# W_down's product as seven products of quarters, with sums of W_down's quarters parked in DRAM

## The chip, the cores and the metric

One core of a Trainium2 chip runs the whole layer; everything is float32 at the interface. The metric is the device time of one execution in microseconds (us), lower is better. Engines are named as in the profile: PE (matrix product), PEld (its weight loads), DVE, ACT, POOL (the compute engines beside it) and SP (which here only issues DMAs).

## The reference, cut to what matters

One layer of a decoder: an attention and convolution block (unchanged here) and then a SwiGLU block and a final norm. The last two lines are what the change touches; S = 512 rows, D_MODEL = 1024, D_FF = 2816.

```python
h = h + mix @ w_o[l]
n = rmsnorm(h, g_ffn[l])
h = h + (jax.nn.silu(n @ w_gate[l]) * (n @ w_up[l])) @ w_down[l]
return rmsnorm(h, g_final)
```

With A = silu(n W_gate) * (n W_up), of 512 x 2816, the change is about A W_down, where W_down is 2816 x 1024.

## The kernel before

**Three products for one.** PE multiplies in fp32r. Each operand is split into a high part (rounded to fp32r by ACT: `wh`, `nH`, `aH`) and a low part (the operand less its high part, by DVE: `wl`, `nL`, `aL`). The helper `mm` (L119 to L121) issues three matmuls for each tile product: high by high, then the two of high and low. `wchunk` loads a weight chunk of 128 x 1024 with a DMA from SP into `raw` and splits it into `wh` and `wl`; `raw`, `wh` and `wl` have three buffers each, so that a chunk's split can run once PE has left the chunk three before it.

**The end of the program, in order.** The product with W_o and the second norm give n in transposed form as `nH`, `nL` (8 tiles of 128 x 512). Then comes gate and up: for each of the FT = 22 tiles ft of D_FF, 24 matmuls of 512 columns with a chunk of W_gate and 24 with a chunk of W_up, each into a PSUM bank (eight of them, `acc`); `ffn_act` (L912) then makes silu (ACT), the product (DVE, L915), and the split of the result into `aH`, `aL` (ACT L916, DVE L917). Its first three chunks are split early into space that `aH` and `aL` take later (`early_chunk`). Then W_down: `wd_mm` (L932) takes an A tile as the stationary operand and W_down's chunk as the moving one, first for the left 512 output columns and all four row tiles t, then for the right 512. `add_sq` adds to `h1` and sums the squares, `var` and a POOL power make 1/rms, and `scale_out` scales and stores.

**Order.** PE's order is the one in which the code is written. The other engines' instructions are ordered ahead of time by a list scheduler; each engine then runs its own list strictly in order, waiting at semaphores. DMAs issued from SP, ACT or POOL stand in that engine's list as well.

Of the kernel before, what the change touches and what calls it, by code (L numbers as in the profile page):

```python
# [51 lines left out]
def trace(tc, a):  # L52
# [879 lines left out]
    def wd_mm(ps, w, fc, t, c0, n):  # L932
        ts_ = slice(t * P, (t + 1) * P)
        for ff in range(2):
            k = 2 * fc + ff
            c = slice(ff * 512 + c0, ff * 512 + c0 + n)
            mm(ps, (aH[:, k, ts_], aL[:, k, ts_]), (w[0][:, c], w[1][:, c]),
               k == 0, k == FT - 1)

    def add_sq(ps, t, cs, q):  # L940
        nc.vector.tensor_tensor(h1[:, t, cs], ps, h1[:, t, cs], op=ALU.add)
# [9 lines left out]
    NF = FT // 2  # L951
    half = slice(0, 512)
    pss = [acc.tile([P, S], F32, name="acc") for _ in range(NT)]
    for fc in range(NF):
        w = wchunk(a["wd"][0, fc], eng=nc.vector)
        for t in range(NT):
            wd_mm(pss[t], w, fc, t, 0, 512)
    for t in range(NT):
        add_sq(pss[t], t, half, 0)
        var(t, 0, EPS)  # L960
        nc.gpsimd.tensor_tensor(h1[:, t, half], h1[:, t, half], gfin[:, half], op=ALU.mult)  # L961


    parts = [(t, 0, 512) for t in range(3)] + [(3, 0, 256), (3, 256, 256)]
    pss = [acc.tile([P, S], F32, name="acc") for _ in parts]

    def part(i, ws, f0):
        t, c0, n = parts[i]
        for q, w in enumerate(ws):
            wd_mm(pss[i][:, 0:n], w, f0 + q, t, c0, n)  # L970

    for fc in range(NF - 2):
        w = wchunk(a["wd"][1, fc], eng=nc.vector)
        for i in range(5 if fc < NF - 3 else 3):
            part(i, [w], fc)
    ws = [w] + [wchunk(a["wd"][1, fc], eng=nc.vector) for fc in range(NF - 2, NF)]

    rest = slice(512, D)

    def scale_out(t):  # L980
        r = st[:, t, 1:2]
        lo, hi = h1[:, t, half], h1[:, t, rest]
# [7 lines left out]
        nc.sync.dma_start(a["out_0"][t][:, rest], hi)  # L990

    for i, (t, c0, n) in enumerate(parts):
        if i < 3:
            part(i, ws[1:], NF - 2)
        else:
            part(i, ws, NF - 3)
        q = 1 if i < 4 else 2
        add_sq(pss[i][:, 0:n], t, slice(512 + c0, 512 + c0 + n), q)
        if i in (1, 2, 4):
            scale_out(t - 1)  # L1000
        var(t, q, st[:, t, 0:1])
        if i != 3:
            nc.gpsimd.tensor_tensor(st[:, t, 1:2], st[:, t, 0:1], mhalf[:, 0:1], op=ALU.pow)
# [74 lines left out]
```

## Time and profile before

| | us |
|---|---|
| median of 3 runs | 919.27 |
| lowest, highest | 918.22, 921.02 |
| the profiled execution, its own time | 917.53 |
| its span, first to last instruction | 915.7 |
| PE busy in the span | 898.8 (98%) |

The profiled execution is one run of its own: its time lies 1.74 us below the median of the three, and 1.83 us of it lies outside the span. Instruction times in the trace count from the span's start. A busy share says how long an engine had an instruction in hand, not that it ran at its best rate.

### The profile page before, as it was taken

Reading aid. Unit: us, or ns where it says so; the run is one execution under the profiler, and the core shown is the slowest. Engines: PE = TensorE matmul, PEld = TensorE weight load, DVE = VectorE, ACT = ScalarE, POOL = GpSimd, SP = SyncE. Lnnn points to the kernel's source line nnn. Section 1 sums busy time; section 2 is a strip of 40 time slices with the busy share of each in tenths; the row PEclk is TensorE's granted clock in tenths of the full one; section 3 lists DMA queues with packets and bytes.
Section 4 is the critical chain, followed back from the end, with each engine's and each line's share of the span. In section 5 each row is a group of like instructions: output and inputs, shape, how many; then the busy total and the mean of one; then the engine's idle time right before and its main releaser. Section 6 shows DMA issues by size and latency. Waiting matters only on the chain.

```text
span 915.7 us, 12776 instructions
## 1 busy us (share of the span) xinstructions
PE 898.8 (98%) x4757; PEld 760.2 (83%) x4757; DVE 515.5 (56%) x1217; ACT 426.3 (47%) x936; POOL 119.6 (13%) x79
## 2 busy tenths in 40 slices
PE   9889999999999999999999999999999999999996
PEld 7789788888888888878888999888888888888885
DVE  4896788888888788775455452333333333223223
ACT  6446776767767777664333522332223222212212
POOL 1000424232242222330000300000000000000100
PEclk9999999999999999999999999999999999999999
DMA  9244511211112111114523700223333323332212
GB/s 313 70 119 162 161 47 50 67 47 53 65 46 71 47 52 65 47 64 150 178 92 97 235 16 24 93 92 92 100 108 92 92 93 103 102 94 92 93 47 92
DMA packets 26270, 85.14 MB, mean 93 GB/s; under 512 B 3424, under 2 KB 3680, under 8 KB 26208
## 3 DMA queue, kind: packets, MB, share of 16 engines
q1 hardware_dynamic: 24912, 82.78, 28.5%
q10 hardware_dynamic: 1296, 1.55, 0.5%
q8 instruction: 37, 0.61, 0.3%
q14 instruction: 25, 0.20, 0.1%
HBM read 82.23 MB, written 2.10 MB: 92 GB/s over the span
## 4 chain that ended last, share of the span: by engine, by line
PE 88%; DVE 6%; DMA 2%; ACT 2%; issue 1%; SPq 0%; POOL 0%; POOLq 0%; ACTq 0%; DVEq 0%
PE acc L119 24%; PE acc L121 24%; PE acc L120 24%; PE sc L497 4%; PE tp L564 4%; PE av L582 2%; PE av L583 2%; DVE blk L249 2%; DVE wl L96 1%; PE av L577 1%; DMA w2kr<-w2k 1%; DMA raw<-wk 1%; ACT wh L95 1%; DMA xT<-xT 0%; DMA xt<-x 0%
## 5 line engine op out<-in xcount | busy, mean ns | idle before, releaser
L95 ACT ACTIVATE wh<-raw 128x1024 fp32r<-128x1024 f32 (+2 forms) x143 | 144.6, 1013 | 314.4 <-PE acc L120 117.0
L119 PE MATMUL acc<-nH,wh 128*128 128x512 f32 x656 | 262.3, 400 | 0.0
L121 PE MATMUL acc<-nH,wl 128*128 128x512 f32 x656 | 256.1, 390 | 0.0
L120 PE MATMUL acc<-nL,wh 128*128 128x512 f32 x656 | 256.1, 390 | 0.0
L96 DVE TENSOR_TENSOR wl<-raw,wh 128x1024 fp32r<-128x1024 f32 (+2 forms) x107 | 123.4, 1154 | 170.1 <-ACT wh L95 170.0
L121 PEld LDWEIGHTS acc<-nH,wl 128*128 128x128 f32 x656 | 123.1, 188 | 26.8 <-POOL wl L96 0.4
L119 PEld LDWEIGHTS acc<-nH,wh 128*128 128x128 f32 x656 | 123.4, 188 | 21.4
L120 PEld LDWEIGHTS acc<-nL,wh 128*128 128x128 f32 x656 | 123.5, 188 | 21.2
L96 POOL TENSOR_TENSOR wl<-raw,wh 128x1024 fp32r<-128x1024 f32 x36 | 86.6, 2407 | 236.7 <-DVE pt L540 96.4
L121 PE MATMUL acc<-wh,aL 128*128 128x512 f32 (+1 forms) x198 | 73.4, 371 | 0.0
L119 PE MATMUL acc<-wh,aH 128*128 128x512 f32 (+1 forms) x198 | 73.4, 371 | 0.0
L120 PE MATMUL acc<-wl,aH 128*128 128x512 f32 (+1 forms) x198 | 73.4, 370 | 0.0
L524 ACT ACTIVATE pt<-pt,nm 128x128 f32<-128x128 f32 (+3 forms) x128 | 70.7, 554 | 2.6 <-DVE nm L509 2.0
L509 DVE CUSTOM_DVE_ANT_0 pt<-sc,tri,nrs 128x128 f32<-128x128 f32 (+3 forms) x128 | 65.4, 545 | 0.1
L568 DVE TENSOR_TENSOR tl<-tp,th 128x512 fp32r<-128x512 f32 x80 | 55.1, 689 | 13.0 <-ACT th L567 11.3
L915 DVE TENSOR_TENSOR sg<-acc,sg 128x512 f32<-128x512 f32 x22 | 15.2, 691 | 81.0 <-PE acc L121 81.0
L567 ACT ACTIVATE th<-tp 128x512 fp32r<-128x512 f32 x80 | 47.4, 592 | 13.2 <-PE tp L564 12.1
L564 PE MATMUL tp<-ident,pt 128*128 128x128 f32 x320 | 49.7, 277 | 0.1
L961 POOL TENSOR_TENSOR h<-h,gfin 128x512 f32<-128x512 f32 x4 | 6.0, 1542 | 299.1 <-ACT jk L943 299.1
L120 PEld LDWEIGHTS acc<-wl,aH 128*128 128x128 f32 x198 | 37.3, 188 | 7.1
L119 PEld LDWEIGHTS acc<-wh,aH 128*128 128x128 f32 x198 | 37.3, 188 | 7.1
L121 PEld LDWEIGHTS acc<-wh,aL 128*128 128x128 f32 x198 | 37.3, 188 | 7.0
(229 smaller groups left out, 1496.9 us busy)
## 6 DMA issues: line engine op xcount, KB each, us to landing
raw<-wg SPq DMA_DIRECT2D x22, 512.0 KB, 3.5
raw<-wu SPq DMA_DIRECT2D x22, 512.0 KB, 3.5
raw<-wd SPq DMA_DIRECT2D x22, 512.0 KB, 3.5
raw<-wcv SPq DMA_DIRECT2D x12, 512.0 KB, 3.6
raw<-wq SPq DMA_DIRECT2D x8, 512.0 KB, 3.6
raw<-w SPq DMA_DIRECT2D x8, 512.0 KB, 3.5
raw<-wgc SPq DMA_DIRECT2D x8, 512.0 KB, 3.5
raw<-wga SPq DMA_DIRECT2D x8, 512.0 KB, 3.5
```

Of the source, the lines that this page charges most:

```text
L95: nc.scalar.activation(h[:, :n], raw[:, :n], AF.Copy)
L96: ins = (eng or nc.gpsimd).tensor_tensor(l[:, :n], raw[:, :n], f(h[:, :n]), op=ALU.subtract)
L119: nc.tensor.matmul(ps, lhs[0], rhs[0], start=first, stop=False)
L120: nc.tensor.matmul(ps, lhs[0], rhs[1], start=False, stop=False)
L121: nc.tensor.matmul(ps, lhs[1], rhs[0], start=False, stop=last)
L249: nc.vector.tensor_tensor(blk[lp * HD:(lp + 1) * HD, :, 2 * ct + hp, 0:NB - 1], src, pos, op=ALU.add)
L497: nc.tensor.matmul(o, q[:, h, qs], kk[g // 2][:, g % 2, c0:c0 + n], start=(j == 0), stop=(j == 1))
L509: nc.vector.tensor_tensor_reduce(out=pt[:, r0:r0 + w].rearrange("p (j c) -> p j c", c=P), in0=sv[:, b], in1=tri[:, NT - 1 - i:NT], scale=n ...
L524: nc.scalar.activation(s, s, AF.Exp, scale=-1.0, bias=nm[:, b:b + 1], accum_out=U[u]["sm"][:, h, b:b + 1])
L564: nc.tensor.transpose(tp[:, (2 * b + h) * P:(2 * b + h + 1) * P], pts[h][:, r0:r0 + P], ident)
L567: nc.scalar.activation(th, tp, AF.Copy)
L568: nc.vector.tensor_tensor(tl, tp, f(th), op=ALU.subtract)
```

## The change

A (as 512 x 2816) is cut into four quarters, by 256 rows and 1408 columns; W_down into four quarters `b11`, `b12`, `b21`, `b22` of 1408 x 512; the output into four of 256 x 512. Instead of eight products of quarters, seven are made (`PRODS`), each of a quarter of A or a difference of two by a quarter of W_down or a sum or difference of two; each product is added to or subtracted from one or two quarters of the output. Three things come with it.

First, the five sums of W_down's quarters are made while gate and up run. In each of 11 rounds `sums(k)` loads four pieces of 128 x 512 with DMAs from POOL, DVE adds them (five instructions) and five DMAs from POOL store them into `scr`, a tile in DRAM. The pieces lie in the two buffers `n2` (named 6102, which holds b11 and b12, and 6103, which holds b21 and b22), three of the sums go in place there and two into `gffn`.

Second, A is kept as plain float32 (`a_`), and a splitted quarter or difference lies in `aC`, which has two slots. `ffn_act` fills the slots of the first two products; `prep_a` makes the others while the product before is on PE.

Third, W_down's chunks come from `scr` or from W_down itself: 42 of them, six for each product (the sixth is a half). All but the first three are split into slots of `nH` and `nL`, which are free after gate and up (`prep_w`).

```diff
+    aC = fp.tile([P, 2, 2, NK, 256], F32R, name="aC")
...
-        r = slice(FT - 2 * q - 2, FT - 2 * q)
-        h, l = [t[:, r].rearrange("p f s -> p (f s)") for t in (aH, aL)]
+        h = eyp.tile([P, 1024], F32R, name=f"ey{q}")
+        l = aCf[:, (10 - q) * 1024:(11 - q) * 1024]
...
     def ffn_act(ft, pg, pu):
         sg = fp.tile([P, S], F32, name="sg", bufs=2)
         nc.scalar.activation(sg, pg, AF.Silu)
-        nc.vector.tensor_tensor(sg, pu, sg, op=ALU.mult)
-        nc.scalar.activation(aH[:, ft], sg, AF.Copy)
-        nc.vector.tensor_tensor(aL[:, ft], sg, f(aH[:, ft]), op=ALU.subtract)
+        a = a_[:, ft]
+        nc.vector.tensor_tensor(a, pu, sg, op=ALU.mult)
+        if ft < NK:
+            part_a(0, ft, 1, a[:, lo])
+            d = fp.tile([P, S], F32, name="sg", bufs=2)[:, lo]
+            nc.vector.tensor_tensor(d, a[:, hi], a[:, lo], op=ALU.subtract)
+            part_a(1, ft, 1, d)
...
+    stg = [fp.tile([P, D], F32, name="n2", bufs=2) for _ in range(2)]
+
+    def sums(k):
+        cs = slice(k * 512, (k + 1) * 512)
+        b = [stg[i // 2][:, (i % 2) * 512:(i % 2 + 1) * 512] for i in range(4)]
+        for i in range(4):
+            nc.gpsimd.dma_start(b[i], a["wd"][i // 2, i % 2][:, cs])
+        o = [gffn[:, 0:512], gffn[:, 512:D]]
+        b11, b12, b21, b22 = b
+        for n, out, x, y in (("11+12", o[0], b11, b12), ("12+22", b12, b12, b22),
+                             ("11-22", o[1], b11, b22), ("11+21", b11, b11, b21),
+                             ("21+22", b22, b21, b22)):
+            nc.vector.tensor_tensor(out, x, y,
+                                    op=ALU.subtract if "-" in n else ALU.add)
+            nc.gpsimd.dma_start(scr[SUMS[n]][:, cs], out)
...
         ffn_act(ft, pg, pu)
+        if 2 <= ft < 2 + NK:
+            sums(ft - 2)
...
+    PRODS = [((0, 0), None, "12+22", [(0, 1, 1), (1, 1, 1)]),
+             ((1, 0), (0, 0), "11+12", [(1, 1, 1)]),
+             ((1, 1), (1, 0), "11", [(1, 0, -1), (1, 1, 1)]),
+             ((0, 1), (0, 0), "22", [(0, 1, 1), (0, 0, -1)]),
+             ((0, 0), (1, 1), "11-22", [(0, 0, 1), (1, 1, 1)]),
+             ((1, 1), None, "11+21", [(0, 0, 1), (1, 0, 1)]),
+             ((0, 1), (1, 1), "21+22", [(0, 0, 1)])]
...
+    def prep_w(n):
...
+        if n < 3:
+            wq_[n] = wchunk(src, w, nc.vector)
+            return
+        nm = ("raw", "wh", "wl")[n % 3]
+        raw = wp.tile([P, 1024], F32 if nm == "raw" else F32R, name=nm)
+        raw = raw if nm == "raw" else f(raw)
+        nc.sync.dma_start(raw[:, :w], src)
+        r = slice(2 * (n % 4), 2 * (n % 4) + 2)
+        h, l = [t[:, r].rearrange("p k c -> p (k c)") for t in (nH, nL)]
+        nc.scalar.activation(h[:, :w], raw[:, :w], AF.Copy)
+        nc.vector.tensor_tensor(l[:, :w], raw[:, :w], f(h[:, :w]), op=ALU.subtract)
+        wq_[n] = h, l
+
+    def prep_a(i, piece):
...
+        if m is not None:
+            d = fp.tile([P, D], F32, name="n2", bufs=2)[:, 0:n * 256]
...
+            nc.vector.tensor_tensor(d, x, a_[:, m[1] * NK + k:m[1] * NK + k + n, TH[m[0]]],
+                                    op=ALU.subtract)
+            x = d
+        h, l = [aC[:, i % 2, e, k:k + n] for e in range(2)]
+        nc.scalar.activation(h, x, AF.Copy)
+        nc.vector.tensor_tensor(l, x, f(h), op=ALU.subtract)
...
+    for i in range(len(PRODS)):
+        last = i == len(PRODS) - 1
+        pss = [acc.tile([P, S], F32, name="acc") for _ in (PARTS if last else PARTS2)]
+        for q in range(NQ - 3 if last else NQ):
+            n = i * NQ + q
+            prep_w(n + AHEAD)
+            for ps, (u, c0, c1, _) in zip(pss, PARTS if last else PARTS2):
+                wd_mm(ps, n, u, c0, c1)
+            if q % 2:
+                prep_a(i + 1, q // 2)
...
+        for u in range(2):
+            for r, c, sign in PRODS[i][3]:
+                evac(pss[u], u, r, c, sign)
```

The layout of `wd` in DRAM changes with it (quarters, so that a piece of a quarter is 128 rows of 2 KB).

What stands on DVE in gate and up, for one tile ft, before (`wl`: the low part of a chunk; L915, L917: `ffn_act`):

```order
L915 TENSOR_TENSOR sg_6188<-acc_6163,sg_6188 128x512
L96 TENSOR_TENSOR wl_6263<-raw_6260,wh_6262 128x1024
L917 TENSOR_TENSOR aL_5355<-sg_6188,aH_5354 128x512
L96 TENSOR_TENSOR wl_6294<-raw_6291,wh_6293 128x1024
L915 TENSOR_TENSOR sg_6255<-acc_6230,sg_6255 128x512
```

And now, in a later round (L933, L937, L943: `ffn_act` and `part_a`; L957: `sums`):

```order
L933 TENSOR_TENSOR a_6101<-acc_6360,sg_6385 128x512
L937 TENSOR_TENSOR sg_6390<-a_6101 128x256
L96 TENSOR_TENSOR wl_6496<-raw_6493,wh_6495 128x1024
L943 TENSOR_TENSOR aC_5357<-a_6101,aC_5357 128x256
L943 TENSOR_TENSOR aC_5357<-sg_6390,aC_5357 128x256
L957 TENSOR_TENSOR gffn_5349<-n2_6102 128x512
L957 TENSOR_TENSOR gffn_5349<-n2_6102,n2_6103 128x512
L957 TENSOR_TENSOR n2_6102<-n2_6102,n2_6103 128x512 x2
L957 TENSOR_TENSOR n2_6103<-n2_6103 128x512
L96 TENSOR_TENSOR wl_6527<-raw_6524,wh_6526 128x1024
L933 TENSOR_TENSOR a_6101<-acc_6445,sg_6470 128x512
```

The five sums of a round stand between two splits of weight chunks: round k, made by `sums(k)`, stands behind the A tile of ft = k - 1 and ahead of the split of W_up's chunk for ft = k + 1. Nothing behind them on DVE can start before they are through.

POOL has nothing in that stretch before: its rows go from the second norm (L810) to the work behind W_down's left half (L961).

```order
L810 TENSOR_TENSOR st<-st,mhalf 128x1 x4
L961 TENSOR_TENSOR h_5346<-h_5346,gfin 128x512 x4
L1003 TENSOR_TENSOR st<-st,mhalf 128x1 x4
L1074 UNCONDITIONAL_BRANCH
L1074 ISA
```

Now it holds the DMAs of the 11 rounds there, one round being (the five stores of a round, then the four loads of the next, L959 and L951):

```order
L959 DMA scr_6096<-gffn_5349 128x512 x2
L959 DMA scr_6096<-n2_6102 128x512 x2
L959 DMA scr_6096<-n2_6103 128x512
L951 DMA n2_6103<-wd 128x512
L951 DMA n2_6102<-wd 128x512 x2
L951 DMA n2_6103<-wd 128x512
```

Three of the four loads overwrite a piece that a store just ahead of them still reads, so they wait until that store has landed.

On DVE where W_down's product begins, before, there are only splits of chunks:

```order
L917 TENSOR_TENSOR aL<-sg,aH 128x512
L96 TENSOR_TENSOR wl<-raw,wh 128x1024 x10
L941 TENSOR_TENSOR h_5346<-acc,h_5346 128x512 x2
L948 TENSOR_SCALAR st<-ssq 128x1
L941 TENSOR_TENSOR h_5346<-acc,h_5346 128x512
```

And now (L1006: a chunk's low part; L1018: a difference of A's quarters; L1023: its low part; L1051: `evac`):

```order
L1006 TENSOR_TENSOR nL_87<-raw_7681,nH_86 128x1024
L1006 TENSOR_TENSOR nL_87<-raw_7729,nH_86 128x1024
L1023 TENSOR_TENSOR aC_5357<-n2_7809,aC_5357 128x1024
L1018 TENSOR_TENSOR n2_7875<-a_6101 128x768
L1006 TENSOR_TENSOR nL_87<-wh_7697,nH_86 128x1024
L1006 TENSOR_TENSOR nL_87<-wl_7713,nH_86 128x512
L1023 TENSOR_TENSOR aC_5357<-n2_7845,aC_5357 128x1024
L1006 TENSOR_TENSOR nL_87<-wh_7745,nH_86 128x1024
L1018 TENSOR_TENSOR n2_7915<-a_6101 128x1024
L1006 TENSOR_TENSOR nL_87<-wl_7761,nH_86 128x1024
L1051 TENSOR_TENSOR h1_5346<-h1_5346,acc_7679 128x512 x2
L1051 TENSOR_TENSOR h1_5346<-h1_5346,acc_7680 128x512 x2
```

The L1023 rows stand ahead of splits of chunks that the product on PE itself still needs (`wh_7697` and `wl_7713` are the product's fifth and sixth chunk), and wait until PE has left the part of `aC` that they write.

## Rows read from the trace of the kernel before

**Rows 1.** The page: busy time by engine; shares of the chain that ended last.
```profile
PE 898.8 (98%) x4757; PEld 760.2 (83%) x4757; DVE 515.5 (56%) x1217; ACT 426.3 (47%) x936; POOL 119.6 (13%) x79
...
PE 88%; DVE 6%; DMA 2%; ACT 2%; issue 1%; SPq 0%; POOL 0%; POOLq 0%; ACTq 0%; DVEq 0%
```

**Rows 2.** Busy time by stretch: gate and up; W_down (columns as headed).
```profile
core 0: us, PE busy (x) PEld busy (x) DVE busy (x) ACT busy (x) POOL busy (x), PEclk, DMA share, GB/s
560.00:780.00 220.00, 220.00 (x980) 182.46 (x979) 74.24 (x80) 63.50 (x81) 0.00 (x0) 1.00 0.30 94
785.00:898.00 113.00, 113.00 (x532) 93.08 (x531) 29.36 (x30) 24.01 (x29) 6.03 (x4) 1.00 0.26 80
```

**Rows 3.** PE in order of time (start us, us, what), around the stages' border.
```profile
779.69 0.39 PE L121 MATMUL acc<-nH,wl 128*128 128x512 f32 x1
...
784.45 0.39 PE L121 MATMUL acc<-nH,wl 128*128 128x512 f32 x1
784.68 0.39 PE L119 MATMUL acc<-wh,aH 128*128 128x512 f32 x1
...
791.94 0.40 PE L120 MATMUL acc<-wl,aH 128*128 128x512 f32 x1
```

**Rows 4.** PE in order of time: 256 columns in W_down, and the last matmul.
```profile
862.00 0.28 PE L119 MATMUL acc<-wh,aH 128*128 128x256 f32 x1
...
863.29 0.28 PE L121 MATMUL acc<-wh,aL 128*128 128x256 f32 x1
...
908.35 0.28 PE L121 MATMUL acc<-wh,aL 128*128 128x256 f32 x1
```

**Rows 5.** DVE in order of time, two tiles of gate and up.
```profile
573.59 1.23 DVE L96 TENSOR_TENSOR wl<-raw,wh 128x1024 fp32r<-128x1024 f32 x1 [3.61 <-ACT wh L95]
...
589.11 0.69 DVE L915 TENSOR_TENSOR sg<-acc,sg 128x512 f32<-128x512 f32 x1 [3.37 <-PE acc L121]
...
599.99 0.69 DVE L915 TENSOR_TENSOR sg<-acc,sg 128x512 f32<-128x512 f32 x1 [3.37 <-PE acc L121]
```

**Rows 6.** DVE, then ACT, by line and shape from 440 us (xcount | busy us, mean ns).
```profile
L96 DVE TENSOR_TENSOR wl<-raw,wh 128x1024 fp32r<-128x1024 f32 x75 | 92.5, 1234 | 160.8 <-ACT wh L95 160.7
L917 DVE TENSOR_TENSOR aL<-sg,aH 128x512 fp32r<-128x512 f32 x22 | 15.1, 685 | 0.7 <-ACT aH L916 0.7
L814 DVE TENSOR_TENSOR h<-acc,h 128x256 f32<-128x256 f32 x16 | 6.4, 418 | 10.3 <-PE acc L121 10.2
...
L95 ACT ACTIVATE wh<-raw 128x1024 fp32r<-128x1024 f32 x75 | 79.6, 1061 | 281.6 <-PE acc L120 106.2 <-issue 85.6 <-PE acc L121 81.2
```

**Rows 7.** POOL by line and shape from 440 us.
```profile
L961 POOL TENSOR_TENSOR h<-h,gfin 128x512 f32<-128x512 f32 x4 | 6.0, 1542 | 299.1 <-ACT jk L943 299.1
L810 POOL TENSOR_TENSOR st<-st,mhalf 128x1 f32<-128x1 f32 x4 | 2.2, 542 | 25.2 <-DVE st L808 25.2
```

**Rows 8.** DMA issues by line (KB each, median us from issue to landing).
```profile
raw<-wg SPq DMA_DIRECT2D x22, 512.0 KB, 3.5
...
raw<-wc SPq DMA_DIRECT2D x8, 256.0 KB, 4.2
...
out<-h SPq DMA_DIRECT2D x7, 256.0 KB, 2.0
```

**Rows 9.** Busy time by stretch, where the DMA engines are busiest, and at a thin PE.
```profile
15.00:20.00 5.00, 5.00 (x24) 4.14 (x23) 2.56 (x5) 4.51 (x9) 0.91 (x1) 1.00 0.98 353
...
40.00:50.00 10.00, 7.47 (x47) 7.25 (x46) 9.77 (x15) 5.12 (x8) 0.00 (x0) 0.83 0.17 53
```

**Rows 10.** POOL, PE and DVE in order of time, around the last transposes.
```profile
545.20 0.54 POOL L810 TENSOR_TENSOR st<-st,mhalf 128x1 f32<-128x1 f32 x1 [6.08 <-DVE st L808]
...
549.49 1.04 PE L838 MATMUL acc<-ident,n 128*128 128x128 f32 x8
550.28 0.37 PE L119 MATMUL acc<-nH,aH 128*128 128x256 f32 x1
...
550.75 1.29 DVE L843 TENSOR_TENSOR nL<-acc,nH 128x512 fp32r<-128x512 f32 x2 [3.69 <-ACT nH L842]
```

More of the change, by code (lines that the diff above doesn't have):

```diff
@@ L930, in trace @@
         ffn_act(ft, pg, pu)
[L932 to L941, printed above, removed]
+        if 2 <= ft < 2 + NK:
+            sums(ft - 2)
@@ new lines, in trace @@
+    PRODS = [((0, 0), None, "12+22", [(0, 1, 1), (1, 1, 1)]),
[6 rows of a table added]
+    NQ = (NK + 1) // 2
+    chunks = [(i, q) for i in range(len(PRODS)) for q in range(NQ)]
+    wq_ = {}
+    def prep_w(n):
+        if n >= len(chunks):
+            return
+        i, q = chunks[n]
+        b = PRODS[i][2]
+        w = 512 * min(2, NK - 2 * q)
+        src = scr[SUMS[b]] if b in SUMS else a["wd"][int(b[0]) - 1, int(b[1]) - 1]
+        src = src[:, q * 1024:q * 1024 + w]
+        if n < 3:
+            wq_[n] = wchunk(src, w, nc.vector)
+            return
+        nm = ("raw", "wh", "wl")[n % 3]
[7 more added lines that the diff above has]
+        wq_[n] = h, l
@@ L942, in add_sq, with wd_mm, square @@
+    def wd_mm(ps, n, u, c0, c1):
+        i, q = chunks[n]
+        w = wq_[n]
+        for kk in range(min(2, NK - 2 * q)):
+            k = 2 * q + kk
+            at = [aC[:, i % 2, e, k, u * P:(u + 1) * P] for e in range(2)]
+            c = slice(kk * 512 + c0, kk * 512 + c1)
+            mm(ps[:, c0:c1], at, (w[0][:, c], w[1][:, c]), k == 0, k == NK - 1)
+    def square(t, cs, q):
         jk = lp.tile([P, S], F32, name="jk", bufs=2)
@@ L949, in var @@
                                 op0=ALU.mult, op1=ALU.add)
[L951 to L978, printed above, removed]
+    def rpow(t):
+        nc.gpsimd.tensor_tensor(st[:, t, 1:2], st[:, t, 0:1], mhalf[:, 0:1], op=ALU.pow)
@@ L980, in scale_out, with evac @@
+    CH = (slice(0, 512), slice(512, D))
+    def evac(ps, u, r, c, sign):
+        t = 2 * r + u
+        nc.vector.tensor_tensor(h1[:, t, CH[c]], h1[:, t, CH[c]], ps,
+                                op=ALU.add if sign > 0 else ALU.subtract)
     def scale_out(t):
         r = st[:, t, 1:2]
-        lo, hi = h1[:, t, half], h1[:, t, rest]
-        if t == 2:
-            nc.vector.tensor_scalar(lo, lo, r, None, op0=ALU.mult)
-        else:
-            nc.scalar.activation(lo, lo, AF.Copy, scale=r)
@@ L987, in scale_out @@
-        (nc.scalar if t == 0 else nc.sync).dma_start(a["out_0"][t][:, half], lo)
-        nc.vector.scalar_tensor_tensor(hi, in0=hi, scalar=r, in1=gfin[:, rest],
+        x, y = h1[:, t, CH[1]], h1[:, t, CH[0]]
+        if t < 2:
+            nc.scalar.activation(x, x, AF.Copy, scale=r)
+        else:
+            nc.vector.scalar_tensor_tensor(x, in0=x, scalar=r, in1=gfin[:, CH[1]],
+                                           op0=ALU.mult, op1=ALU.mult)
+        (nc.scalar if t == 1 else nc.sync).dma_start(a["out_0"][t][:, CH[1]], x)
@@ L989, in scale_out @@
+        nc.vector.scalar_tensor_tensor(y, in0=y, scalar=r, in1=gfin[:, CH[0]],
                                        op0=ALU.mult, op1=ALU.mult)
[L990 to L1003, printed above, removed]
@@ L1004, in trace @@
-    scale_out(3)
+        nc.sync.dma_start(a["out_0"][t][:, CH[0]], y)
+    PARTS2 = ((0, 0, 512, 0), (1, 0, 512, 0))
+    PARTS = ((0, 0, 512, 1), (1, 0, 256, 1), (1, 256, 512, 2))
+    AHEAD = 3
+    for n in range(AHEAD):
+        prep_w(n)
+    for i in range(len(PRODS)):
[8 more added lines that the diff above has]
+                prep_a(i + 1, q // 2)
+        if last:
+            break
+        for u in range(2):
+            for r, c, sign in PRODS[i][3]:
+                evac(pss[u], u, r, c, sign)
+        for u in range(2):
+            if i == 3:
+                square(u, CH[1], 0)
+                var(u, 0, EPS)
+                nc.gpsimd.tensor_tensor(h1[:, u, CH[1]], h1[:, u, CH[1]], gfin[:, CH[1]],
+                                        op=ALU.mult)
+            elif i == 4:
+                square(2 + u, CH[1], 0)
+                var(2 + u, 0, EPS)
+            elif i == 5:
+                square(2 + u, CH[0], 1)
+                var(2 + u, 1, st[:, 2 + u, 0:1])
+                rpow(2 + u)
+                scale_out(2 + u)
@@ L1005, in trace @@
+    for ps, (u, c0, c1, q) in zip(pss, PARTS):
+        for n in range(len(chunks) - 3, len(chunks)):
+            wd_mm(ps, n, u, c0, c1)
+        cs = slice(c0, c1)
+        nc.vector.tensor_tensor(h1[:, u, cs], h1[:, u, cs], ps[:, cs], op=ALU.add)
+        square(u, cs, q)
+        if q == 1 and u == 1:
+            scale_out(0)
+        var(u, q, st[:, u, 0:1])
+        if (u, q) != (1, 1):
+            rpow(u)
+    scale_out(1)
     es.close()
@@ L1059, in layout @@
     o["wo"] = o["wo"].reshape(4, 2, P, 1024)
-    o["wd"] = o["wd"].reshape(2, FT // 2, P, 1024)
+    o["wd"] = o["wd"].reshape(2, 2, P, FT // 2 * 512)
     return o
```

26 lines of the change are left out of this document (23 added, 3 removed).

## The prediction

> **What bounds the kernel now.** I read the page first, for the busy shares and the chain of work that ended last: PE is busy for 98% of the span and owns 88% of the chain [rows 1], so time is to be won only by less work on PE, and is lost wherever PE is made to wait. Then the stretches: in gate and up, and in W_down, PE has no gap at a granted clock of 1.00 (the upper of the two levels, 2.4 GHz), while DVE is busy 74.2 of 220 us and 29.4 of 113 us, and POOL not at all in gate and up [rows 2]. So DVE, POOL and the DMA engines have room there; the question is whether what the change puts on them keeps its due times. Then PE in order of time, for the pitch of a matmul: 21 starts in 4.76 us before the border (0.2267 us each) and 31 in 7.26 us after it (0.2342 us each) [rows 3]; with 256 columns, 11 in 1.29 us, 0.117 us each [rows 4].
>
> **What the change removes.** W_down takes 22 x 4 x 2 x 3 = 528 matmuls of 512 columns (some as two of 256, whose pitch is half). Seven products take 7 x 11 x 2 x 3 = 462. The 66 that go save 66 x 0.2342 = 15.5 us. The stage check: 528 x 0.2342 = 123.7 us, and from its first start, 784.68, to its last, 908.35, are 123.7 us [rows 3, 4]. At the other pitch for all 462 it would be 18.9 us; the stationary operand is still A and the moving one W_down, as in the rows with 0.2342, so I take 15.5.
>
> **What it adds in gate and up.** A tile ft lasts 599.99 - 589.11 = 10.88 us [rows 5]. DVE has two splits, one product and one low part in it now, 2 x 1.234 + 2 x 0.69 = 3.8 us. It will have two splits, the product, three of 256 columns (0.418 each) and five sums (by the nearest rows 0.69 each, also if both inputs are in SBUF, as in L917): 7.9 us [rows 6]. It fits; ACT gains less. Work is not the issue, order is: the sums wait for DMAs, and the split behind them waits for the sums.
>
> So I follow one round. From the issue of a round's second store to that of the next round's, POOL issues eight DMAs (four stores, four loads); the last load lands; DVE makes the sum that needed it (0.69); POOL issues. A DMA of 256 KB lands 2.0 us after its issue where the queue is quiet [rows 8]. What an issue occupies POOL for, no row shows. Its own smallest instruction takes 0.54 us, and one over 128 x 512 elements 1.54 us [rows 7]; an issue moves no element but writes something for each of 128 rows, so I take the middle, 1.0. The round is then 8 x 1.0 + 2.0 + 0.69 = 10.7 us; by the two ends 7.0 and 15.0. There is a second floor, the DMA engines: a round moves nine times 262 KB and, meanwhile, two weight chunks of 524 KB, 3.41 MB. The best stretch shows 353 GB/s [rows 9], so 9.7 us; gate and up shows 94 GB/s at a share of 0.30, or 313 GB/s if the share were full [rows 2], so 10.9 us. With some queueing I take 11.4 us for the round.
>
> What can it last before PE waits? The split of W_up's chunk for ft = 3 started at 573.59 and PE began with that chunk half a tile before the end of ft = 3, at 589.1 - 5.4 = 583.6 [rows 5]. It now stands behind round 2, and in each later round the like. The one behind round 10 must be done by 583.6 + 8 x 10.88 = 670.6, so round 10 by 669.4. Round 0 can load its last two pieces once PE has transposed the last n2, at 550.3 [rows 10]: two issues, 2.0 us, four sums, so it ends at about 557. Ten rounds have 112.4 us, **11.2 us each**. Each us above that costs PE 10 us. At 11.4 this is 2 us; I take 2, from 0 (any round under 11.2) to 38 (15.0).
>
> The Trainium skill, in "DMA: Bandwidth & Descriptors" (Anatomy of one DMA), gives a DMA from POOL a fixed 2.0 us and its bytes over 436 GB/s, which is 2.6 us for 256 KB, an estimate by that page; no run so far shows one. By it a round is 0.6 us longer, and the sum would come out 6 us higher, near 913.
>
> At the first round, POOL's loads stand behind its power at 545.20 to 545.74, and DVE now has round 0's first sum ahead of the last nL (550.75, done at 552.04). PE needs that nL after 24 matmuls of 0.117 us from 550.28, at 553.1 [rows 4, 10], so 1.0 us is spare. Two issues and 2.0 us put the loads at 549.8, the sum at 550.5: no cost; with 1.54 us an issue, 0.2 us. I take 0, up to 3 if POOL's first DMA is late.
>
> **What it adds in W_down.** PE needs 462 x 0.2342 = 108.2 us. DVE has 32 splits of 1024 columns and seven of 512 (44.3 us), five low parts of A's quarter (two of 1.234 and one of 768 columns, about 0.96: 17.1), four differences (13.7), 24 additions (16.7), and some 6 of scaling: 98 us, 90% of PE's [rows 6]. By product it is uneven: the third and fourth need 6.9 + 6.9 + 2.8 = 16.5 us against 15.5 of PE. Walking down DVE's order with these times, I find each split ready about 1 us or more before PE wants it. The first tight one: the fifth chunk's split stands behind a low part of A, which waits for PE to leave its second chunk (24 x 0.2342 = 5.6 us in) and for ACT's high part (1.06); with that low part, a difference and the split itself it is ready at 5.6 + 1.06 + 1.23 + 0.96 + 1.23 = 10.1 us, and PE wants it after four chunks of 12, at 11.2. So I take 1 us, from 0 to 6 (a wait of 1 us at each of six borders). The chunks' DMAs double their rate to some 187 GB/s, far from 353. The tail is alike: evacuation, square, power, scale, store. I take 0, give or take 1.
>
> **The sum.** 917.5 - 15.5 + 2 + 0 + 1 + 0 = 905.0 us for an execution like the profiled one; the median lies 1.7 above it, so **907 us**, 1.4% faster.
>
> **The rivals.**
> - *POOL's issues are the bound (slower).* At 1.54 us an issue the round is 15.0 us and the sums cost 38 us: 907 + 36 = 943. It decides from 8e + 2.7 = 12.7, e = 1.25 us an issue: there the waits eat the 15.5 us. For it: it is only a quarter of a us above what I took, and every us is paid ten times. Against: POOL does nothing else there. PE's clock could add to it: where PE was busy only 7.47 of 10 us, the granted clock was 0.83 [rows 9].
> - *The DMA engines are the bound.* At 313 GB/s and with the round's own idle trip of 1.4 us, a round is 12.3 us, 11 us in all instead of 2: 916. If loads land in 4.2 us, as 256 KB did under a full queue [rows 8], it is 8 + 4.2 + 0.7 = 12.9 us, 17 us: 922. Against: the weight chunks come in bursts, and the first store of a round need not wait for the last load.
> - *DVE holds POOL off.* If an issue had to wait for the DVE instruction in progress (half of 1.2 us on average, DVE being busy 7.9 of 10.9 us), an issue of 1.0 would be about 1.4, a round 13.9, and the sums 27 us: 932. The Trainium skill, "SBUF — State Buffer" (Who interferes with whom), says that a DMA issued on POOL starves while DVE runs an instruction that takes both ports, and that tensor_tensor was not seen to do so. By that page this rival falls here, since DVE's rows in this stretch are all of that kind [rows 5]; no run yet shows it.
> - *W_down turns DVE-bound.* Its order leaves 1 us at the tightest places. If PE waited 1 to 2 us at each of the six borders between products: 6 to 12 us, 912 to 918.
> - *It doesn't do what it says.* The order shows 99 matmuls fewer (33 of 512 and 66 of 256 columns), so the saving is there.
>
> **Chances.** Rounds keep up within 6 us: 0.58. DMA-bound at 914 to 922: 0.14. W_down bound by DVE: 0.06. POOL-bound or held off, beyond 917: 0.22. Likeliest case alone: 902 to 911. A change under 0.3% (2.8 us) is about what this kernel's timing can't tell from none. Faster by more (under 916.5): 0.58, nearly all of W_down's 0.06 and about half of the DMA's, 0.70 in all. Within: 0.09. Slower (over 922): the rest of POOL's, 0.21. For the range I leave 0.05 below 902 (the 18.9 us saving, or no queueing at all) and about 0.13 above 927.
>
> **What the profile after should show.** W_down at 108 us at a pitch of 0.234. Tiles of gate and up still 10.88 us apart, with DVE idle before L957 ended by a DMA, and the idle before PE near zero. POOL's issues in gate and up in a row: their distance is e. It is wrong if tiles ft = 2 to 11 stretch to over 11.2 us with PE waiting for `wl` or `wh`; if L1006 or L1023 ends PE's waits in W_down; or if round 0 delays the last nL.

## The result, and the profile after

The changed kernel takes 926.62 us (median of 9 runs, 923.97 to 931.0), the kernel before 920.14 (9 runs on the same chips): a ratio of 1.0073, 95% interval 1.0058 to 1.0089. It is slower by 0.7%. Forecast were 907 us. The profiled execution took 924.03 us, its span is 922.2, so 6.5 us more than before (both profiled executions lie 2.6 us below their medians).

The page of the kernel after, busy time and the chain, to be read against [rows 1]:
```profile
PE 890.3 (97%) x4658; PEld 749.9 (81%) x4658; DVE 605.2 (66%) x1347; ACT 452.0 (49%) x970; POOL 172.6 (19%) x176
...
PE 73%; DMA 12%; DVE 6%; issue 3%; POOL 3%; ACT 1%; SPq 0%; POOLq 0%; DVEq 0%; ACTq 0%
```
PE has 99 matmuls less and is busy 8.5 us less, but owns 73% of the chain where it had 88%; DMAs, which had 2%, have 12%. Something waits for transfers.

Where? PE around the border of gate and up to W_down, and its last matmul, after [rows 3, 4]:
```profile
802.24 0.39 PE L121 MATMUL acc<-nH,wl 128*128 128x512 f32 x1
802.47 0.39 PE L119 MATMUL acc<-wh,aC 128*128 128x512 f32 x1
...
910.63 0.28 PE L121 MATMUL acc<-nH,aC 128*128 128x256 f32 x1
```
W_down takes 910.63 - 802.47 = 108.2 us instead of 123.7: the 15.5 us are there. But W_down begins 17.8 us later than before, and the span ends 922.2 - 910.63 = 11.6 us behind the last matmul instead of 7.35. Of the 17.8 us, 1.8 come from earlier in the program: the last transposes begin at 551.32 instead of 549.49 (in experiment 6, which has the change, at 549.86), and the kernels part between 60 and 80 us, where both run the same instructions at another granted clock (windows of before, then of after):
```profile
60.00:80.00 20.00, 17.15 (x129) 16.33 (x127) 12.40 (x22) 9.39 (x20) 0.00 (x0) 1.00 0.41 132
```
```profile
60.00:80.00 20.00, 17.43 (x121) 16.81 (x120) 11.31 (x21) 8.01 (x16) 0.00 (x0) 0.91 0.40 128
```
So the account of the 6.5 us is -15.5 (W_down) + 16.0 (gate and up) + 4.2 (end) + 1.8 (not the change's).

Gate and up and W_down by stretch, after [rows 2] (same columns):
```profile
580.00:600.00 20.00, 17.59 (x77) 14.24 (x76) 12.47 (x19) 4.44 (x7) 8.54 (x16) 0.99 0.65 227
600.00:620.00 20.00, 20.00 (x83) 16.36 (x83) 9.55 (x16) 6.38 (x10) 6.13 (x12) 0.92 0.81 287
620.00:640.00 20.00, 16.95 (x74) 13.37 (x73) 13.87 (x22) 5.60 (x9) 9.24 (x17) 1.00 0.73 254
...
660.00:680.00 20.00, 17.36 (x69) 13.54 (x68) 11.20 (x18) 5.59 (x9) 8.01 (x15) 0.91 0.79 261
...
700.00:780.00 80.00, 80.00 (x354) 66.27 (x353) 25.50 (x24) 18.88 (x23) 0.00 (x0) 1.00 0.33 97
803.00:908.00 105.00, 105.00 (x471) 85.49 (x470) 87.63 (x99) 55.75 (x67) 6.21 (x4) 1.00 0.54 178
```
PE has gaps only while the rounds run (to 700 us); behind them and in all of W_down it has none, though DVE is busy 87.6 of 105 us there. Where PE has had gaps, the granted clock is at times below 1.00 in the mean, so not always on the upper of its two levels (0.92 at 600 to 620 us, 0.91 at 660 to 680). The waits between 560 and 700 us (total, times, longest) say who is late:
```profile
POOL scr L959 <- DVE gffn L957: 53.2, 17, 6.5
DVE gffn L957 <- issue: 37.5, 7, 6.4
...
POOL n L951 <- DMA scr<-n: 17.7, 19, 2.0
DVE gffn L957 <- DMA n<-wd: 16.4, 9, 5.2
...
PE acc L121 <- DVE wl L96: 10.6, 7, 2.4
```
From the bottom: PE waits 10.6 us for splits, which stand on DVE behind sums, which wait for loads, which POOL issues once stores have landed. (DVE's 37.5 us have no releaser in the view, but in rounds 2 to 10 the first sum begins about 0.1 us after a load has landed.) Of the rest of the 16.0 us, 5.4, some 3 are PE running slower behind a wait: from 600 to 620 us it is busy throughout at a mean clock of 0.92 and starts 83 matmuls, where 90 fit at 1.00, a loss of 1.6 us, and from 660 to 680 us the clock is 0.91. The last 2 us these rows don't divide. One round on POOL in order of time, then the sums on DVE that let the next round's stores go:
```profile
620.54 0.54 POOL L959 DMA_DIRECT2D scr<-gffn  x1 [5.07 <-DVE gffn L957]
622.05 0.54 POOL L959 DMA_DIRECT2D scr<-gffn  x1 [0.96 <-DVE gffn L957]
622.65 1.74 POOL L959 DMA_DIRECT2D scr<-n  x3
624.39 0.55 POOL L951 DMA_DIRECT2D n<-wd  x1
625.56 0.55 POOL L951 DMA_DIRECT2D n<-wd  x1 [0.62 <-DMA scr<-n]
626.58 0.55 POOL L951 DMA_DIRECT2D n<-wd  x1 [0.47 <-issue]
628.23 0.55 POOL L951 DMA_DIRECT2D n<-wd  x1 [1.11 <-DMA scr<-n]
633.05 0.54 POOL L959 DMA_DIRECT2D scr<-gffn  x1 [4.27 <-DVE gffn L957]
634.33 0.54 POOL L959 DMA_DIRECT2D scr<-gffn  x1 [0.74 <-DVE gffn L957]
```
```profile
632.06 0.69 DVE L957 TENSOR_TENSOR gffn<-n 128x512 f32<-128x512 f32 x1 [4.50 <-DMA n<-wd]
633.34 0.69 DVE L957 TENSOR_TENSOR gffn<-n,n 128x512 f32<-128x512 f32 x1 [0.59 <-DMA n<-wd]
```
An issue takes 0.55 us. The loads go out one by one over 4.4 us as the stores land, and 4.3 us pass from the last issue's end to the next round's first store. From second store to second store, as the prediction counts, that is 2.3 us until the first load is issued (622.05 to 624.39), 3.8 until the last is (628.23), 5.1 until it has landed and the second sum begins (633.34), and 1.0 to the store: 12.3 us. From the first store of round 0 (552.46) to that of round 10 (684.47) are 132.0 us: 13.2 us a round. The DMA issues, after [rows 8]:
```profile
raw<-wg SPq DMA_DIRECT2D x22, 512.0 KB, 4.2
...
n<-wd POOLq DMA_DIRECT2D x44, 256.0 KB, 5.1
scr<-n POOLq DMA_DIRECT2D x33, 256.0 KB, 2.8
...
scr<-gffn POOLq DMA_DIRECT2D x22, 256.0 KB, 2.3
```
At the end, the instructions of the program's closing line (count, ns least, median, most; first and last start):
```profile
L1184 POOLq DRAIN  x3: 40/102/8756, 912.4 to 922.0; - x3
```
And before:
```profile
L1074 POOLq DRAIN  x3: 34/77/636, 910.3 to 915.5; - x3
```
The longest of the three, POOL's drain, takes 8.76 us from 912.4 on, though POOL's last DMA went out near 690. Before, it took 0.64 us and the end waited for the last output instead.

### The profile page after: what moved, and what is told of

The parts are those of the page before. It is cut to its first block, busy times and chain, and to the rows that moved or that the text cites. A ratio compares the mean times of both kernels' runs of the same rounds, so it can differ in the third digit from the quotient of the medians.

```text
span 922.2 us, 13016 instructions
## 1 busy us (share of the span) xinstructions
PE 890.3 (97%) x4658; PEld 749.9 (81%) x4658; DVE 605.2 (66%) x1347; ACT 452.0 (49%) x970; POOL 172.6 (19%) x176
## 4 chain that ended last, share of the span: by engine, by line
PE 73%; DMA 12%; DVE 6%; issue 3%; POOL 3%; ACT 1%; SPq 0%; POOLq 0%; DVEq 0%; ACTq 0%
PE acc L121 19%; PE acc L119 19%; PE acc L120 19%; DMA n<-wd 6%; PE sc L497 4%; PE tp L564 4%; DMA scr<-n 3%; PE av L582 2%; PE av L583 2%; POOL scr L959 2%; DVE blk L249 2%; PE av L577 1%; DVE wl L96 1%; DVE gffn L957 1%; DMA w2kr<-w2k 1%
## 5 line engine op out<-in xcount | busy, mean ns | idle before, releaser
L121 PE MATMUL acc<-nH,wl 128*128 128x512 f32 x656 | 258.4, 394 | 10.9 <-DVE wl L96 10.6
L95 ACT ACTIVATE wh<-raw 128x1024 fp32r<-128x1024 f32 (+2 forms) x124 | 124.4, 1004 | 191.0 <-PE acc L120 135.0
L96 DVE TENSOR_TENSOR wl<-raw,wh 128x1024 fp32r<-128x1024 f32 (+2 forms) x88 | 100.1, 1139 | 59.2 <-ACT wh L95 58.2
L121 PE MATMUL acc<-nH,aC 128*128 128x512 f32 (+1 forms) x201 | 71.6, 356 | 0.0
L568 DVE TENSOR_TENSOR tl<-tp,th 128x512 fp32r<-128x512 f32 x80 | 55.2, 690 | 13.0 <-ACT th L567 11.2
L120 PE MATMUL acc<-nL,aC 128*128 128x512 f32 (+1 forms) x153 | 58.1, 380 | 0.0
L119 PE MATMUL acc<-nH,aC 128*128 128x512 f32 (+1 forms) x153 | 58.1, 380 | 0.0
L567 ACT ACTIVATE th<-tp 128x512 fp32r<-128x512 f32 x80 | 47.4, 592 | 13.2 <-PE tp L564 12.1
L540 DVE TENSOR_SCALAR pt<-pt,fac 128x128 f32<-128x128 f32 (+3 forms) x128 | 42.9, 380 | 0.0
L121 PEld LDWEIGHTS acc<-nH,aC 128*128 128x128 f32 x201 | 37.9, 188 | 6.0
L564 PEld LDWEIGHTS tp<-ident,pt 128*128 128x128 f32 x320 | 36.3, 140 | 7.4 <-DVE pt L540 0.3
L524 ACT ACTIVATE pc<-pc,nm 128x32 f32<-128x32 f32 x64 | 20.5, 320 | 44.5 <-DVE nm L504 44.0
L957 DVE TENSOR_TENSOR gffn<-n 128x512 f32<-128x512 f32 x11 | 7.6, 692 | 52.5 <-issue 37.5
```

Source lines behind the costliest of these rows:

```text
L95: nc.scalar.activation(h[:, :n], raw[:, :n], AF.Copy)
L96: ins = (eng or nc.gpsimd).tensor_tensor(l[:, :n], raw[:, :n], f(h[:, :n]), op=ALU.subtract)
L119: nc.tensor.matmul(ps, lhs[0], rhs[0], start=first, stop=False)
L120: nc.tensor.matmul(ps, lhs[0], rhs[1], start=False, stop=False)
L121: nc.tensor.matmul(ps, lhs[1], rhs[0], start=False, stop=last)
L524: nc.scalar.activation(s, s, AF.Exp, scale=-1.0, bias=nm[:, b:b + 1], accum_out=U[u]["sm"][:, h, b:b + 1])
```

## The experiments

"A round" is the distance of the first stores of consecutive rounds, on average. The times of before are those of the same chip, 919.4 to 920.5 us.

**1. No sums.**
```diff
-        if 2 <= ft < 2 + NK:
-            sums(ft - 2)
...
-        src = scr[SUMS[b]] if b in SUMS else a["wd"][int(b[0]) - 1, int(b[1]) - 1]
+        src = a["wd"][int(b[0]) - 1, int(b[1]) - 1]
```

> Leaves out the five sums of W_down's quarters and all their DMAs; each product reads a plain quarter of W_down instead, so its output differs. All else of the change stays. Theory (the rounds of loads and stores are too slow by about 2 us each, and their being issued from POOL costs about 4 us at the program's end): both losses go, before less 15.5 us = about 904.6, PE's end to the span's end back at about 7.4 us, no gap of PE in gate and up. Rival 1 (the loss in gate and up comes from the other new instructions of that stage, the plain A and the two slots of aC): gate and up stays about 16 us longer, 919 to 921. Rival 2 (the longer end comes from the new tail, not from POOL's DMAs): end stays at 11.6 us, 909.

904.67 us, ratio 0.983 (0.9812 to 0.9847), and 6.9 us from PE's last matmul to the end. As expected: both losses belong to the sums; the new `ffn_act` and the new W_down cost nothing.

**2. Half the pace.**
```diff
+        tile_done[ft] = nc.vector.tensor_tensor(a, pu, sg, op=ALU.mult)
...
+            ins = nc.gpsimd.dma_start(b[i], a["wd"][i // 2, i % 2][:, cs])
+            if k:
+                tc.add_manual_dep(inst(ins), inst(tile_done[2 * k - 1]).name,
...
-        if 2 <= ft < 2 + NK:
-            sums(ft - 2)
+        if ft % 2:
+            sums(ft // 2)
```


> All of the computation is there; a round of sums every second tile of gate and up (21.8 us for each) instead of every tile, nothing else changed. Theory (a round's chain of landings lasts about 13 us whatever comes of it; the loss is only what it exceeds a tile by): gate and up is back at its length, the 4 us at the end stay, 920.1 - 15.5 + 4.2 = about 909 (907 to 911). Rival (the total work of the sums costs it: bytes beside the weights, DVE, PE's granted clock): the same work spread still costs most of its 16 us, 918 to 926.

908.48 us, 0.9877 (0.9861 to 0.9893). PE has no wait in gate and up, its clock is 1.00 in every stretch, and the end stays at 11.6 us. Loads land in 3.4 us.

**3. A quarter of the bytes.**
```diff
+            m = 512 if k == 0 else 128
+            nc.gpsimd.dma_start(b[i][:, 0:m], a["wd"][i // 2, i % 2][:, cs][:, 0:m])
...
+            nc.gpsimd.dma_start(scr[SUMS[n]][:, cs][:, 0:m], out[:, 0:m])
```

> From the second round on, the sums' DMAs move 128 of 512 columns (a quarter of the bytes, the same count of DMAs and of rows); the products read plain quarters of W_down, so the output differs. Theory a (a landing of 5.1 us is bytes and queueing beside the weight chunks): landings fall to 2 to 3 us, a round to about 9 us, gate and up loses nothing, 909. Theory b (a landing is a fixed trip of POOL's queue and 128 descriptors, whatever the bytes): landings stay above 4 us, rounds above 12 us, 920 to 926.

916.29 us, 0.9957 (0.9944 to 0.9971): between the two. Stores land in 1.8 us, loads in 3.2, a round is 10.8 us, a tile's pace; PE still waits 5.0 us in three places, and sums stand at other, partly earlier places on DVE's list here. Bytes are part of a landing, not all of it.

**4. One DMA from POOL in the kernel before.**
```diff
-    nc.scalar.dma_start(convw, a["conv_w"])
+    nc.gpsimd.dma_start(convw, a["conv_w"])
```

> The kernel before, with one small DMA at the program's start (the convolution's weights) issued from POOL instead of ACT; nothing else. Theory (using POOL's DMAs at all makes the program's end about 4 us longer): PE's end to the span's end goes from 7.4 to about 11.6 us, 924. Rival (the longer end comes from the number of POOL's DMAs, or from the new order of the tail): no change, 920.

919.92 us, 1.0001 (0.999 to 1.0012). My theory of the end fell: having a DMA on POOL costs nothing. The drain took 0.735 us with one DMA, 0.64 without, and 8.76 with 99 in kernels 2 and 3 as well, whatever their bytes and whenever the last one went out. That suggested a price for each.

**5. Sums out of place.** Three buffers `o3` take the sums that lay on their inputs.
```diff
-        for n, out, x, y in (("11+12", o[0], b11, b12), ("12+22", b12, b12, b22),
-                             ("11-22", o[1], b11, b22), ("11+21", b11, b11, b21),
-                             ("21+22", b22, b21, b22)):
+        for n, out, x, y in (("11+12", o[0], b11, b12), ("12+22", o3[0], b12, b22),
+                             ("11-22", o[1], b11, b22), ("11+21", o3[1], b11, b21),
+                             ("21+22", o3[2], b21, b22)):
```

> The three sums that overwrote their own inputs go to buffers of their own, so that no load waits for a store of the same piece; every tile still has its round. Theory (the loop of a round is store landing, load landing and sums in a row; 3 to 4 us of its 13 are the store's landing): rounds come down to about 9.5 us where DVE allows it, under the 11.2 us, PE's waits for the low part of a chunk go, 909 (908 to 913). Rival (DMA engines or POOL's queue set the rhythm): a load waits as long elsewhere, rounds stay at 12 to 13 us, 920 to 926.

934.58 us, 1.0163 (1.0144 to 1.0182): it missed by 25 us, on the wrong side. Rounds are 12.6 us: without the wait for the store's landing they are 0.6 us shorter, not 3 to 4. PE waits 15.1 us in six places, and its clock is 0.83 to 0.93 in the mean in four of the five stretches of 20 us from 600 to 700 us. POOL, then DVE, in order of time:
```profile
608.15 0.54 POOL L962 DMA_DIRECT2D scr<-st  x1
608.68 1.63 POOL L954 DMA_DIRECT2D n<-wd  x3
```
```profile
615.44 0.69 DVE L960 TENSOR_TENSOR gffn<-n 128x512 f32<-128x512 f32 x1 [6.45 <-DMA n<-wd]
616.05 0.68 DVE L933 TENSOR_TENSOR a<-acc,sg 128x512 f32<-128x512 f32 x1
```
The loads now go out together with the stores and need 5.1 us from the last issue's end (610.31) to the sum. And the scheduler put the first sum ahead of the tile's product (L933), so more stands behind it. Two things changed, then, and the run doesn't divide the loss between them.

**6. Sums on POOL, and 7. the same with the first differences moved** (the last two lines).
```diff
-            nc.vector.tensor_tensor(out, x, y,
+            nc.gpsimd.tensor_tensor(out, x, y,
...
+            if i == 2:
+                tc.add_manual_dep(inst(ins), inst(tile_done[FT - 2]).name,
...
```

> The five sums of a round are made by POOL instead of DVE; loads, stores and their places stay. Theory (rounds hurt only because the sums stand ahead of the splits on DVE's list): rounds get longer than 13 us, by about 5 x (1.54 - 0.69) = 4 us, and PE still has no wait in gate and up as long as 11 rounds of 18 to 20 us end before W_down begins: 909 (908 to 913). Rival (the rounds hurt by their traffic, through the weight chunks' landings or PE's clock): 918 to 926, and longer if W_down's first chunk waits for the last round.

> The five sums made by POOL, as in the run before, and the first differences of A's quarters for W_down's third product (DVE, into the buffers that the rounds use) put behind the tile ft = 20 on DVE's list. There one such difference stood on DVE's list at 710 us, waited for the last round's stores until 733 and held the splits behind it: PE waited 15.0 us once. Theory (rounds of some 17 us cost nothing as long as nothing on an in-order list that PE needs stands behind them): no wait of PE in gate and up, 925.5 - 15.0 - 1.5 (lower clock behind the wait) = about 909, of which 4 us are the end. Rival (something in the traffic of the rounds costs PE time anyway): the 15 us come back elsewhere, 918 to 925.

6: 925.5 us, 1.0055 (1.0037 to 1.0074). Rounds are 17.2 us, PE has no gap until 700 us, and then one of 15.0. On DVE:
```profile
732.93 1.23 DVE L1018 TENSOR_TENSOR n<-a 128x1024 f32<-128x1024 f32 x1 [23.08 <-DMA scr<-n]
734.07 2.35 DVE L96 TENSOR_TENSOR wl<-raw,wh 128x1024 fp32r<-128x1024 f32 x2
```
A difference that needs the rounds' buffers waits 23 us, with the splits behind it. 7: 907.59 us, 0.9871 (0.9854 to 0.9887), with no gap of PE. Two of its windows:
```profile
600.00:620.00 20.00, 20.00 (x90) 16.57 (x89) 10.49 (x12) 6.81 (x10) 12.28 (x16) 1.00 0.72 239
620.00:640.00 20.00, 20.00 (x90) 16.54 (x90) 12.45 (x12) 5.26 (x8) 11.59 (x14) 1.00 0.71 247
```
The traffic is somewhat less than the changed kernel's (239 and 247 GB/s against 287 and 254), loads land as late (5.0 us), rounds are longer (17.3 us), and PE loses nothing. So late loads and long rounds don't cost PE time by themselves: they do where sums stand ahead of splits on DVE's list. (That more traffic costs none either, 12 shows.)

**8. A round every 13.6 us.** `PACE` names, for a tile, the round and whether it begins at mid-tile.
```diff
...
+        if ft in PACE:
+            k, mid = PACE[ft]
+            sums(k, u_split if mid else tile_done[ft - 1])
...
```

> All as in the spread kernel with its DMAs from POOL, but a round begins every two and a half chunks, 13.6 us, instead of every 21.8. Theory (a round needs 13 us beside the weights, and the loss is only what it exceeds its allotted time by): almost no wait of PE, 909 to 912. Rival (the loss grows with the sums' share of the DMA traffic, so that 0 us at 21.8 and 16 us at 10.9 go with something between at 13.6): 915 to 920.

916.5 us, 0.9971 (0.9955 to 0.9987), PE waits 5.1 us in three places; rounds came 14.9 us apart. Missed, and inside the rival's range. 7 and 12 speak against that rival, with 215 to 319 GB/s between 580 and 660 us and no loss; my reading, which no run here tests by itself, is that an allotted time above a round's average isn't enough, since each single round must come ahead of the split behind it.

**9. Half the weights.** (`half=4`: `dense` takes the k-th tile's weights from the columns of tile k % 4.)
```diff
+            wg = wchunk(a["wg"][ft][:, 0:512], 512, nc.vector)
...
+            dense(pg, wg, nH, nL, half=4)
...
```

> The changed kernel with half of each chunk of W_gate and W_up from ft = 2 on (512 of 1024 columns loaded and split, each used twice, so the output differs); PE's matmuls and the rounds are the same. Theory a (loads of a round land in 5.1 us because they share the DMA engines with weight chunks): loads land in about 4 us, rounds shrink below 12 us, 912 to 918. Theory b (a round's own nine DMAs and their trips make its 13 us): landings and rounds stay, 923 to 927.

915.25 us, 0.9951 (0.9933 to 0.997), rounds 12.3 us, waits 4.1. The time is theory a's, but loads still land in 4.9 us; by this run sharing with the weights is at most about 1 of the 2 us that a round is too long. (The shorter splits on DVE help, too.)

**10. Stores from SP at half pace, and 11. loads as well** (the first two lines in 11 only).
```diff
-            ins = nc.gpsimd.dma_start(b[i], a["wd"][i // 2, i % 2][:, cs])
+            ins = nc.sync.dma_start(b[i], a["wd"][i // 2, i % 2][:, cs])
...
-            nc.gpsimd.dma_start(scr[SUMS[n]][:, cs], out)
+            nc.sync.dma_start(scr[SUMS[n]][:, cs], out)
```

> A round every second tile, and the 55 stores issued from SP instead of POOL, so POOL issues 44 DMAs instead of 99. In the profiles POOL's last drain took 0.64 us with no DMA of POOL, 0.74 with one and 8.76 with 99 (three kernels, whatever their bytes). Theory (the drain grows by 0.082 us for each DMA that POOL issued): it takes 0.64 + 44 x 0.082 = 4.2 us, which the last output's landing hides, and the end is back at 7.4 us: 908.5 - 4.2 = about 904.3. Rival 1 (a step between 1 and 44, then constant): drain 8.76, 908.5. Rival 2 (stores in SP's list hold up weight chunks): PE waits in gate and up, 906 or more.

> A round every second tile, all 99 DMAs of the sums from SP, none from POOL. Theory: the drain is 0.64 us, the end 7.4 us, 904.3, the same as with POOL's 44. Rival (loads and stores that wait in SP's list hold up the weight chunks behind them): PE waits in gate and up, 906 to 915.

10: 904.16 us, 0.9827 (0.9812 to 0.9842). 11: 903.23, 0.9818 (0.9798 to 0.9838). No waits of PE in either. The drain of 10, with 44 DMAs from POOL, and of 11, with none:
```profile
L1193 POOLq DRAIN  x3: 40/93/4262, 896.6 to 902.1; - x3
```
```profile
L1193 POOLq DRAIN  x3: 40/82/651, 895.8 to 900.8; - x3
```
4.26 us where 0.64 + 44 x 0.082 = 4.25 was expected: the price is for each DMA, and shows only beyond the 4 us or so that the last output needs anyway.

**12. The changed kernel, all DMAs of the sums from SP** (both edits of 11, without the pace).

> The changed kernel, a round for every tile, with all 99 DMAs of the sums issued from SP instead of POOL. Theory (the rounds are slow because their bytes and the weight chunks share the DMA engines, and the sums stand on DVE's list ahead of splits; who issues does not matter): rounds stay at about 13 us, the 16 us in gate and up stay, only the end's 4.2 us go: about 922, or more if weight chunks wait behind the sums' DMAs on SP's list. Rival (a DMA issued from POOL lands late by itself): rounds fall to 10 to 11 us, 904 to 908.

902.99 us, 0.981 (0.9794 to 0.9827), no wait of PE: the theory fell, the rival held. Rounds (from round 1) are 11.4 us, at 288 to 319 GB/s between 580 and 660 us, more than POOL's rounds ever moved. But the scheduler also put a split ahead of the sums here, so two things had changed. **13** moves that split in the changed kernel, DMAs from POOL; **14** moves it back, DMAs from SP (13, then 14):
```diff
+            if k:
+                tc.add_manual_dep(inst(ins), inst(u_split[k + 1]).name,
...
```
```diff
+        if ft <= NK:
+            sums(ft - 1)
         wu = wchunk(a["wu"][ft], eng=nc.vector)
+        if 2 <= ft <= NK:
+            tc.add_manual_dep(inst(last_split[0]), inst(last_sum[0]).name,
...
```

> The changed kernel, DMAs from POOL, with one thing moved on DVE's list: from the second round on the split of W_up's chunk stands ahead of the round's sums instead of behind them (the place that it has by itself in the kernel that issues from SP). Theory S (who issues decides: from POOL a round takes 13 us): rounds stay at 12.5 to 13.5 us, and half a tile of slack gives back some 5 of the 16 us once, 915 to 922. Theory O (the place on DVE's list decides): PE's waits go, 907 to 910, of which 4 are the end.

> The kernel that issues from SP, with the split of W_up's chunk put back behind the round's sums on DVE's list, as the changed kernel has it. Theory S: rounds come at a tile's pace, 10.9 us, and PE waits little: 903 to 907. Theory O: PE waits as in the changed kernel, 915 to 922.

13: 919.94 us, 1.0003 (0.9989 to 1.0017), rounds 13.2 us, waits 8.2 us. 14: 903.68 us, 0.9831 (0.9816 to 0.9845), no waits. Theory S: with the same order on DVE's list, rounds are 13.2 us from POOL and 11.0 from SP (the changed kernel and 14), and 13.2 and 11.4 with the split ahead (13 and 12). The split's place gave back about 6 us by the ratios (1.0073 and 1.0003), 4 of them in gate and up of the profiled executions. A round of 14 on SP:
```profile
619.66 0.33 SPq L965 DMA_DIRECT2D scr<-gffn  x1
621.31 0.33 SPq L965 DMA_DIRECT2D scr<-n  x1
621.68 0.43 SPq L965 DMA_DIRECT2D scr<-gffn  x1
622.21 0.97 SPq L965 DMA_DIRECT2D scr<-n  x2
624.58 2.31 SPq L957 DMA_DIRECT2D n<-wd  x4
626.94 0.42 SPq L95 DMA_DIRECT2D raw<-wg  x1
627.46 0.38 SPq L95 DMA_DIRECT2D raw<-wu  x1
630.52 1.55 SPq L965 DMA_DIRECT2D scr<-gffn  x2
```
10.9 us. From the first store to the first load are 4.9 us (3.9 in the changed kernel's round above), the loads go out in 2.3 (4.4), and from there to the next store are 3.6 (4.3). On average of rounds 1 to 10 the largest difference is the last load's landing, 4.3 us after its issue against 5.6. The weight chunks now stand behind the loads in the same list; in the changed kernel SP issued them at 624.73 and 626.92, among the round's loads.

**15. All from ACT** (`nc.scalar` for `nc.gpsimd`), to tell POOL's own cost from that order.

> The changed kernel with the 99 DMAs of the sums issued from ACT, so from a queue that is neither POOL's nor the one in which the weight chunks stand. Theory P (POOL's own issue and landing make the round 13 us): rounds come at 10.9 to 11.5 us, 903 to 908. Theory Q (from SP the loads stand ahead of the weight chunks in one queue, and from any other queue they share the DMA engines with them): loads still land 4 to 5 us after the last issue, rounds 12 to 13 us, 912 to 922. Either is blurred if ACT's high parts wait behind a DMA's wait on ACT's list; then PE waits for ACT's wh.

908.46 us, 0.9879 (0.9862 to 0.9895), PE waits 3.0. The first stores of rounds 1 and 10:
```profile
566.93 0.33 ACTq L959 DMA_DIRECT2D scr<-gffn  x1
...
686.62 0.33 ACTq L959 DMA_DIRECT2D scr<-gffn  x1
```
So a round takes 13.3 us, as from POOL, and the median load lands in 4.2: theory Q's rounds, with a time next to theory P's. It is blurred as feared: high parts of chunks wait on ACT's list behind its DMAs, and splits stand at other places among the sums on DVE's list. It doesn't settle the question, but a long round is not POOL's alone.

## Why the prediction was wrong, point by point

- **W_down, -15.5 us:** right. It took 108.2 us at the pitch of 0.2342, without a wait of PE; the 1 us for DVE's order was not needed, and the rival of a DVE-bound W_down fell.
- **The threshold, 11.2 us a round:** roughly right for the order on DVE's list that it was made for. At 13.2 us it would cost 20 us and cost 16.0; SP's rounds of 11.0 (14) cost none. With other orders it isn't a rule: rounds of 10.8 us made PE wait 5.0 us in 3, rounds of 13.3 only 3.0 in 15.
- **The round, "10.7 us ... With some queueing I take 11.4 us": the step that failed.** It measured 13.2. Two of its terms were off, against each other: an issue of 1.0 us was 0.55, so the eight issues cost 3.6 us less; but one landing of 2.0 us stood for what is two in a row, the stores' landings, for which the loads wait one by one (some 2 us a round; the section on the change names that wait, the working has no term for it), and the loads' own of 5.1. The second is the larger error: with the first wait taken away (5), loads landed later still, in 5.6 us, and rounds were 12.6. The 2.0 came from a quiet queue [rows 8], and this queue isn't quiet: nine DMAs a round, among weight chunks that themselves went from 3.5 to 4.2 us. The row for a full queue, 4.2 us, stood beside it, and the rival made from it (a round of 12.9 us, 922) came nearest; with the end's 4.2 us it is 926. That it comes so near is in part luck: its issues of 1.0 us are 3.6 us too long in sum, its single landing some 3 too short.
- **The tail, "0, give or take 1":** wrong by a term that I had not listed, the drain of POOL's 99 DMAs, +4.2 us. Experiments 4, 10 and 11 put it at 0.082 us for each DMA.
- **POOL's issues as the bound:** the 1.25 us from which this was to decide were not reached. Yet with the same order on DVE's list, rounds issued from SP were short enough and those from POOL were not (14 against the changed kernel, 12 against 13). How much of that is POOL's own way of issuing and how much that its loads share the engines with weight chunks, which in SP's list stand behind them, stays open: 9 gives the weights at most about half, and 15, with rounds of 13.3 us from ACT, leans to the second but is blurred.
- **DVE holds POOL off:** fell. From 560 to 700 us every issue took 0.54 to 0.55 us while DVE was busy up to 13.9 of 20 us. By the Trainium skill, "SBUF — State Buffer" (Who interferes with whom), it had to fall here, and the trace agrees.
- **The estimate for a DMA from POOL:** the Trainium skill, "DMA: Bandwidth & Descriptors" (Anatomy of one DMA), made an estimate of 2.6 us for 256 KB from POOL. The landings of the stores to `scr` between 560 and 700 us:
```profile
DMA to landing us min/median/max: 2.3/2.7/4.8
```
The stores' median agrees roughly; under this kernel's traffic the median load took 5.1. The Trainium skill's price would have made 913; the loss was larger.
- **My first explanation,** after the result, was the loop through the stores (5 didn't bear it out, though DVE's order changed there as well) and then the shared DMA engines alone (12 and 14 refuted it: more traffic, 288 to 319 GB/s, and no loss). What stands: the rounds take 13 us from POOL and 11 from SP, and they cost PE time only through the splits behind them on DVE's list (7).

With the sums' DMAs from SP the change does what was forecast, and more: 903 us, 1.9% faster than before.
